# Two transformer blocks on one core: the residual stream kept as token rows, with output and down projections that hold the activations stationary

## The chip, the cores and the metric

The kernel runs on one core of a Trainium2 chip. The metric is the device time of one execution in microseconds (us). A core has a matrix engine (TensorE, PE in the profile), a vector engine (VectorE, DVE), a scalar engine (ScalarE, ACT), GpSimd (POOL) and a queue engine (SyncE, SP) that here issues the DMA transfers of the weights. Times of one run come from three executions; the profile is one more execution with the hardware profiler on.

## The reference

256 tokens of width 2048 pass two blocks, in float32. Block 1:

```
h = rmsnorm(x, norm_attn_pre);  proj = h @ w_in
mixed = concat(dilated window attention (8 heads), latent attention (8 heads))
x = x + rmsnorm(mixed @ w_out, norm_attn_post)
h = rmsnorm(x, norm_mlp_pre);  u = square(relu(h @ w_up))        # 2048 -> 8192
x = x + rmsnorm(u @ w_down, norm_mlp_post)                       # 8192 -> 2048
```

Block 2:

```
h = rms_norm(x, norm1_g);  proj = h @ w_in_2
mixed = concat(window attention (8 heads), bidirectional gated linear attention (4 heads))
x = x + mixed @ w_out_2
h = rms_norm(x, norm2_g);  u = conv3(h @ w_up_2);  gate, val = split(u)   # 2 x 5632 columns
x = x + (silu(gate) * val) @ w_down_2                                     # 5632 -> 2048
```

Each `rmsnorm` divides a token's 2048 values by the root of their mean square and multiplies by a gain vector, one gain for each channel. Three norms matter here: the one ahead of the first MLP ("norm 2", behind the post-norm of the attention), the one ahead of block 2 ("norm 3", behind the post-norm of the first MLP) and the one ahead of the second MLP ("norm 4").

## The kernel before

Every float32 operand is split in a high and a low part (`hi`, `lo`); a product of two operands is three matmuls: high by high, high by low, low by high. Weights are streamed: a DMA brings a raw tile of four K-chunks (128 rows by 512 columns each; three buffers), ScalarE copies two chunks at a time into `whi` (line 173), VectorE subtracts into `wlo` (line 174); two chunks so split are a "part", and three parts can be held. All projection matmuls are issued by `mm` on line 121, so the profile tells them apart by the name of the accumulation tile:

- `pb` (`proj_b`): the activations of 128 tokens are the stationary operand, 512 weight columns stream past; a K-chunk is 2 token blocks by 3 matmuls of 512 columns, and the result is token rows.
- `pa` (`proj_a`): the weights are stationary, 256 tokens stream past; a K-chunk is 4 x 3 matmuls of 256 columns, and the result is channel rows (channels on partitions).
- `pm` (`proj_m`): weights stationary, channel rows too. With `both`, the high weights meet the high and low activations side by side in one matmul of 512 columns, and the low weights the high activations in one of 256: 4 pairs a chunk. Without it, 12 matmuls of 256 columns.

The residual stream is held as channel rows, `xT`, two tiles of [128, 8, 256]. Both output projections write channel rows: three groups of 512 output channels by `proj_a`, the last one by `proj_m` in its 256-column form. Behind the last one come the sums of squares over channels (`Stats`, with `sps` matmuls against a column of ones), the power on GpSimd (`rstd`, line 180), and two matmuls that spread the row over the partitions (`spread`, tile `spr`). `post_norm` then computes chunk after chunk of the new residual and of `hT`, the normalised activations times the gain (`scaled_split`, lines 211 and 212), while the first matmuls that use them are under way. `hold_back` and `late` keep the first weight splits behind the norm's own instructions.

Each MLP starts with a wide group (1024 columns, 256-column matmuls, eight accumulators); all further up groups and the down projections are `proj_m` pairs, except the last down group, in the 256-column form. Block 1 runs its MLP in four parts of 16 chunks of the hidden width (`sb`), block 2 in three (16, 16, 12): up, then down into four groups, accumulated into `acc` or `xT`.

Attention work is cut in small steps, which a list (`Side`) issues between the parts of a projection (`tick`, `side.rate` steps per part); `flush` issues what is left. The output projection of a block needs the heads in the order of `MK`, four at a time (`need`), and flushes those. Instructions run in program order on each engine, and a scheduler inserts the waits. In block 2 the input projection's parts stand in this order: keys, queries and gates (`ka`, `kb`, `qg`) right behind norm 3, decay gates, the remaining `pb` groups for queries and values (`vg`, two blocks of 512 columns, the last before the output projection).

Of the kernel before, what the change touches and what calls it, by code (L numbers as in the profile page):

```python
# [10 lines left out]
F32 = mybir.dt.float32  # L11
# [8 lines left out]
P = 128  # L20
# [6 lines left out]
G_PRE1, G_CQ, G_CKV, G_POST1, G_PRE2, G_POST2, G_PRE3, G_PRE4, G_BAF, G_BAB, G_CW, G_CB = (  # L27
    0, 16, 20, 24, 40, 56, 72, 88, 104, 108, 112, 112 + 264)
G_N = 112 + 352
# [60 lines left out]
def tile_two_blocks(ctx: ExitStack, tc: tile.TileContext, a: dict, out: bass.AP):  # L90
# [3 lines left out]
    whl = ctx.enter_context(tc.tile_pool(name="whl", bufs=3))  # L94
    big = ctx.enter_context(tc.tile_pool(name="big", bufs=14))
# [3 lines left out]
    psb = ctx.enter_context(tc.tile_pool(name="psb", bufs=5, space=PSUM))  # L99
    pss = ctx.enter_context(tc.tile_pool(name="pss", bufs=3, space=PSUM))  # L100
# [4 lines left out]
    def scratch(shape, name, dt=F32):  # L105
        return scr.tile(shape, dt, tag="t2", name=name, bufs=12)
# [28 lines left out]
    nc.sync.dma_start(gains[:, :G_POST1], a["gains"][:, :G_POST1])  # L135
# [31 lines left out]
    late, held = [None, None], [0, 0]  # L167

    def hold_back():
        held[:] = 1, 2  # L170

# [4 lines left out]
    def rstd(ss, n, width):  # L176
        v = col(n, "v")
        late[1] = nc.vector.tensor_scalar(v, ss, 1.0 / width, EPS, op0=ALU.mult, op1=ALU.add)
        r = col(n, "r")
        nc.gpsimd.tensor_tensor(r, v, mhalf[:, :n], op=ALU.pow)  # L180
        return r
# [32 lines left out]
    def w_parts(nk, n, loads, pieces=1, first=False):  # L214
# [9 lines left out]
        for i in range(nk // h):  # L224
            if first:
                split_xT(i)
            hi = whl.tile([P, h, n], F32R, tag="hi", name="whi")
            lo = whl.tile([P, h, n], F32R, tag="lo", name="wlo")
            with ExitStack() as order:
                if held[0]:  # L230
                    held[0] -= 1
                elif held[1]:
                    held[1] -= 1
                    for ins in late:
                        order.enter_context(tc.issue_after(ins.ins))
                split(hi, lo, raw[:, i * h:(i + 1) * h])
            yield [(i * h + k, hi[:, k], lo[:, k]) for k in range(h)]
            side.tick()

    def proj(xT, ks, loads_of, ktile, before, pieces, body, both=False, final=False):  # L240
        nk = len(ks)
        for k0 in range(0, nk, ktile):
            kk = min(ktile, nk - k0)
            if before is not None:
                before(k0)
            parts = w_parts(kk, *loads_of(ks[k0], kk), pieces=pieces if k0 == 0 else 2 if pieces > 1 and k0 == ktile else 1,
                            first=pieces > 1 and k0 == 0)
            if final and k0 + kk == nk:
                parts = [[e for part in parts for e in part]]
            for part in parts:  # L250
                body([(k0 + k == 0, k0 + k == nk - 1, *hl(xT, ks[k0 + k]),
                       *([hl2(xT, ks[k0 + k])] if both else []), wh, wl) for k, wh, wl in part])

    def proj_b(xT, ks, loads_of, evac, n=512, before=None, pieces=1):
        ps = [bankb(f"pb{tb}") for tb in range(2)]

        def body(part):
            for first, last, xh, xl, wh, wl in part:
                for tb in range(2):
                    s = slice(tb * P, (tb + 1) * P)  # L260
                    o = ps[tb][:, :n]
                    mm(o, xh[:, s], wh, first, False)
                    mm(o, xh[:, s], wl, False, False)
                    mm(o, xl[:, s], wh, False, last)

        proj(xT, ks, loads_of, 4, before, pieces, body)
        for tb in range(2):
            evac(tb, ps[tb])

    def proj_a(xT, ks, loads_of, evac, n=512, ktile=4, before=None, pieces=1):  # L270
# [11 lines left out]
        proj(xT, ks, loads_of, ktile, before, pieces, body)  # L282
# [4 lines left out]
    def proj_m(xT, ks, loads_of, evac, n=512, both=True, before=None, final=False):  # L287
        if n == 512:
            turn[0] ^= both
            ps = [banks(f"pm{b}") if both and turn[0] and b < 3 else bankb(f"pm{b}") for b in range(4)]  # L290
            of = [p[:, :T] for p in ps]
        else:
            ps = [bankb(f"pm{b}") for b in range(4)]
            of = [p[:, m * T:(m + 1) * T] for p in ps for m in range(2)]
        alone = n == 512
        if not alone:
            turn[0] = 0

        def body(part):
            for m, o in enumerate(of):  # L300
                c = slice(m * P, (m + 1) * P)
                for first, last, xh, xl, xb, wh, wl in part:
                    if both:
                        mm(ps[m], wh[:, c], xb, first, last)
                        mm(ps[m][:, T:], wl[:, c], xh, False, last)
                    else:
                        mm(o, wh[:, c], xh, first and (alone or m % 2 == 0), False)
                        mm(o, wh[:, c], xl, False, False)
                        mm(o, wl[:, c], xh, False, last)

        proj(xT, ks, loads_of, 2048 // n, before, 1, body, both=True, final=final)
        for m, o in enumerate(of):
            evac(m, o, ps[m][:, T:] if both else None)
# [52 lines left out]

    def cols2(r):
        return [r[:, 0:1], r[:, 1:2]]
# [96 lines left out]
    nc.sync.dma_start(gains[:, G_POST1:], a["gains"][:, G_POST1:])  # L465
# [224 lines left out]
    xT = [slot([P, 8, T], F32, f"xr{j}") for j in range(2)]  # L690
    for j in range(2):
        nc.sync.dma_start(xT[j], a["xt"][j * 1024:(j + 1) * 1024, :].rearrange("(k p) t -> p k t", p=P))

    def bank3(ps):
        return ps.rearrange("p (m t) -> p m t", t=T)

    class Stats:
        def __init__(self):
            self.i = 0

        def add(self, src):
            i = self.i
            self.i += 1
            if i % 2 == 0:
                self.sq = scratch([P, 2, T], "sq")
            sq = self.sq
            if i == NC - 1 and src.space != PSUM:
                nc.vector.tensor_mul(sq[:, i % 2], src, src)
            else:
                late[0] = nc.scalar.activation(sq[:, i % 2], src, AF.Square)  # L710
            if i == NC - 1:
                token_sum(self.ps, [sq[:, 1]], False, True)
                return self.ps[:, 0:2]
            if i == NC - 2:
                self.ps = banks("sps")
                token_sum(self.ps, [self.acc[:, 0], sq[:, 0]], True, False)
            elif i == 1:
                self.acc = sq
            elif i % 2:
                nc.vector.tensor_add(self.acc, self.acc, sq)  # L720
            if i == NC - 3:
                nc.vector.tensor_add(self.acc[:, 0], self.acc[:, 0], self.acc[:, 1])

    def post_norm(xT, yT, row, g0, dst, wide):
        for c, n in ((0, 1), (1, 1), (2, 1), (3, 1), *((c, 2) for c in range(4, NC, 2))):
            t = scratch([P, n, T], "pn")
# [618 lines left out]
```

## Time and profile before

| | |
|---|---|
| device time, median of 3 | 2194.13 us (2193.82 to 2195.15) |
| the profiled execution | 2196.3 us |
| its span, first to last instruction | 2194.5 us |
| granted TensorE clock, mean | 0.995 |
| busy: PE, DVE, ACT, POOL | 2175.1, 1391.7, 1088.0, 16.0 us |
| DMA | 396.14 MB, mean 181 GB/s |

A clock of 1.00 means that TensorE was granted its full 2.4 GHz, 0.5 that it was at 1.2 GHz. Matmuls overlap: the durations in a row of the timeline overlap their neighbours, and the distance from one start to the next is what a matmul costs in a stream. A piece of the chain of waits that holds many matmuls gives that distance as its length over its count. The last of several matmuls in a piece is followed by the start of the next piece.

### The profile page before, as it was taken

Reading aid. Unit: us, or ns where it says so; the run is one execution under the profiler, and the core shown is the slowest. Engines: PE = TensorE matmul, PEld = TensorE weight load, DVE = VectorE, ACT = ScalarE, POOL = GpSimd, SP = SyncE. Lnnn points to the kernel's source line nnn. Section 1 sums busy time; section 2 is a strip of 40 time slices with the busy share of each in tenths; the row PEclk is TensorE's granted clock in tenths of the full one; section 3 lists DMA queues with packets and bytes.
Section 4 is the critical chain, followed back from the end, with each engine's and each line's share of the span. In section 5 each row is a group of like instructions: output and inputs, shape, how many; then the busy total and the mean of one; then the engine's idle time right before and its main releaser. Section 6 shows DMA issues by size and latency. Waiting matters only on the chain.

```text
span 2194.5 us, 32879 instructions
## 1 busy us (share of the span) xinstructions
PE 2175.1 (99%) x13298; PEld 1943.2 (89%) x13298; DVE 1391.7 (63%) x2115; ACT 1088.0 (50%) x1578; POOL 16.0 (1%) x22
## 2 busy tenths in 40 slices
PE   8999999999999999999999999999999999999999
PEld 8988899988888888888898889998888888888888
DVE  7665565764565565566678775566765567655765
ACT  6554454644443444344466565445553455534553
POOL 0000000000000000000000000000000000000000
PEclk9999999999999999999999999999999999999999
DMA  7545644555655665665454543545555555555555
GB/s 258 164 135 184 201 172 164 170 195 192 191 190 187 187 189 190 191 192 193 146 186 154 176 162 115 182 166 180 191 187 182 188 192 181 184 192 185 180 192 154
DMA packets 249641, 396.14 MB, mean 181 GB/s; under 512 B 12784, under 2 KB 107888, under 8 KB 249488
## 3 DMA queue, kind: packets, MB, share of 16 engines
q1 hardware_dynamic: 249488, 394.03, 55.5%
q8 instruction: 104, 1.70, 0.3%
q14 instruction: 49, 0.40, 0.0%
HBM read 391.90 MB, written 2.10 MB: 180 GB/s over the span
## 4 chain that ended last, share of the span: by engine, by line
PE 96%; DVE 2%; DMA 1%; ACT 1%; issue 0%; POOL 0%; SPq 0%; POOLq 0%; ACTq 0%
PE pm L121 69%; PE pb L121 11%; PE pa L121 8%; PE qg L121 1%; DMA raw<-in_w_in 1%; PE uq L121 1%; PE sc L121 1%; DVE wlo L174 1%; PE ka L121 1%; PE pv L121 1%; PE pk L121 1%; PE kb L121 0%; PE po L121 0%; ACT whi L173 0%; PE wsc L121 0%
## 5 line engine op out<-in xcount | busy, mean ns | idle before, releaser
L174 DVE TENSOR_TENSOR wlo<-raw,whi 128x1024 fp32r<-128x1024 f32 (+2 forms) x758 | 902.8, 1193 | 676.2 <-ACT whi L173 673.4
L173 ACT CAST whi<-raw 128x1024 fp32r<-128x1024 f32 (+2 forms) x758 | 776.6, 1026 | 938.5 <-PE pm L121 700.4
L121 PE MATMUL pm<-hT,whi 128*128 128x512 f32 (+1 forms) x2688 | 860.9, 376 | 2.5 <-ACT hT L211 1.5
L121 PE MATMUL pm<-hT,wlo 128*128 128x256 f32 x2432 | 684.9, 282 | 0.0
L121 PE MATMUL pm<-u,whi 128*128 128x512 f32 (+1 forms) x1840 | 605.2, 381 | 0.0
L121 PEld LDWEIGHTS pm<-hT,whi 128*128 128x128 f32 x2688 | 491.9, 190 | 100.4 <-ACT hT L211 1.7
L121 PE MATMUL pm<-u,wlo 128*128 128x256 f32 x1728 | 484.7, 281 | 0.0
L121 PEld LDWEIGHTS pm<-hT,wlo 128*128 128x128 f32 x2432 | 462.5, 190 | 0.0
L121 PEld LDWEIGHTS pm<-u,whi 128*128 128x128 f32 x1840 | 337.6, 188 | 70.2
L121 PEld LDWEIGHTS pm<-u,wlo 128*128 128x128 f32 x1728 | 326.7, 189 | 0.0
L121 PE MATMUL pb<-whi,hT 128*128 128x512 f32 x768 | 246.0, 395 | 0.1
L121 PEld LDWEIGHTS pb<-whi,hT 128*128 128x128 f32 x768 | 144.2, 188 | 29.5 <-DVE nr_t L892 0.5
L121 PE MATMUL pb<-wlo,hT 128*128 128x512 f32 x384 | 151.4, 394 | 0.2 <-DVE wlo L174 0.2
L121 PE MATMUL pa<-mix,whi 128*128 128x256 f32 x768 | 141.3, 286 | 0.0
L121 PEld LDWEIGHTS pa<-mix,whi 128*128 128x128 f32 x768 | 120.3, 192 | 0.9 <-DVE mix L1196 0.4
L121 PE MATMUL pa<-mix,wlo 128*128 128x256 f32 x384 | 108.5, 284 | 0.1
L121 PEld LDWEIGHTS pb<-wlo,hT 128*128 128x128 f32 x384 | 72.2, 188 | 15.7 <-DVE wlo L174 1.8
L121 PE MATMUL pa<-hT,whi 128*128 128x256 f32 x384 | 72.4, 290 | 5.6 <-ACT whi L173 5.4
L121 PEld LDWEIGHTS pa<-mix,wlo 128*128 128x128 f32 x384 | 73.5, 192 | 0.3 <-DVE wlo L174 0.3
L121 PEld LDWEIGHTS pa<-hT,whi 128*128 128x128 f32 x384 | 61.0, 196 | 7.4 <-ACT whi L173 6.6
L1253 ACT ACTIVATE gv<-us,gains 128x256 f32<-128x256 f32 x80 | 46.0, 601 | 27.9 <-DVE us L1276 27.2
L121 PE MATMUL pa<-hT,wlo 128*128 128x256 f32 x192 | 54.9, 289 | 1.0 <-DVE wlo L174 1.0
(289 smaller groups left out, 1594.6 us busy)
## 6 DMA issues: line engine op xcount, KB each, us to landing
raw<-in_w_down SPq DMA_DIRECT2D x108, 1024.0 KB, 5.0
raw<-in_w_up SPq DMA_DIRECT2D x176, 512.0 KB, 4.1
raw<-in_w_up SPq DMA_DIRECT2D x64, 1024.0 KB, 5.5
raw<-in_w_in SPq DMA_DIRECT2D x62, 1024.0 KB, 5.2
raw<-in_w_out SPq DMA_DIRECT2D x32, 1024.0 KB, 5.1
raw<-in_w_ukv SPq DMA_DIRECT2D x4, 1024.0 KB, 5.1
raw<-in_w_uq SPq DMA_DIRECT2D x4, 768.0 KB, 4.6
raw<-in_w_in SPq DMA_DIRECT2D x4, 544.0 KB, 3.7
```

The source lines that it names most:

```text
L121: nc.tensor.matmul(ps, lhsT, rhs, start=start, stop=stop, skip_group_check=True)
L173: nc.scalar.copy(hi, src)
L174: return nc.vector.tensor_sub(lo, src, hi.bitcast(F32))
L1253: nc.scalar.activation(dst, ps, AF.Identity, bias=b, scale=w[1])
```

## The change

The residual stream is kept as token rows: `xN[tb]`, one tile of [128 tokens, 2048] for each of the two token blocks. `proj_a` stays only in input projections. All projections whose result is added to the residual run as `proj_b`, and the last group of each one that precedes a norm as `proj_last`: its last eight K-chunks (`TRAIL`) are multiplied first for token block 0, then that block is evacuated and its norm is computed (`chain`), then the same eight chunks run for block 1. The normalised rows are transposed by TensorE (`flips`, line 125, tiles `fl`), four 128 x 128 pieces at a time, between the first eight chunks of the next projection, which runs as `proj_first`. The up projections' first group of each MLP is such a `proj_first` too; its output rows are transposed afterwards (`flip_rows`, tiles `fl` and `fu`). All other up groups are `proj_m` pairs. There are 112 such transposes in the program.

The gains of norms 2 and 4 are multiplied into the weights while these are split (`fold`: a `scaled_split` for each K-chunk of 512 columns in place of one `split` for two chunks). The gain of norm 3 is applied in the transposes' copies, in pieces of 128 columns. The gains of the post-norms are rows, broadcast over the partitions (`gp`). Sums of squares come from ScalarE's accumulated `Square` per 512 columns.

In block 2, the first `vg` block is multiplied right behind norm 3 (`proj_first`), the residual is written to DRAM (`x2`) and read back ahead of the second `vg` block, and the gated linear attention's steps are flushed ahead of that one. The split tiles have six buffers in place of three; the pool of 8 KB slots has 12 in place of 14, and that of scratch tiles 10 in place of 12. The output leaves as token rows.

The core of the diff:

```
-    whl = ctx.enter_context(tc.tile_pool(name="whl", bufs=3))
-    big = ctx.enter_context(tc.tile_pool(name="big", bufs=14))
+    whl = ctx.enter_context(tc.tile_pool(name="whl", bufs=6))
+    big = ctx.enter_context(tc.tile_pool(name="big", bufs=12))
...
+            r = raw[:, i * h:(i + 1) * h]
+            if fold is None:
+                split(hi, lo, r)
+            else:
+                for k in range(h):
+                    scaled_split(hi[:, k], lo[:, k], r[:, k], gain(fold + i * h + k))
...
+    TRAIL = LEAD = 8
+
+    def proj_last(xT, ks, loads_of, evac, done0=None, mid=None, before=None):
+        ps = [bankb(f"pb{tb}") for tb in range(2)]
+        held, k = [], 0
+        for part in stream(xT, ks, loads_of, before=before):
+            if k < len(ks) - TRAIL:
+                for e in part:
+                    for tb in range(2):
+                        rows_mm(ps, tb, [e])
+            else:
+                rows_mm(ps, 0, part)
+                held.append(part)
+            k += len(part)
+        evac(0, ps[0])
+        if done0:
+            done0()
+        for i, part in enumerate(held):
+            if i == len(held) - 1 and mid:
+                mid()
+            rows_mm(ps, 1, part)
+        evac(1, ps[1])
+
+    def proj_first(xT, ks, loads_of, flips, evac, n=512, fold=None):
+        ps = [bankb(f"pb{tb}") for tb in range(2)]
+        parts = stream(xT, ks, loads_of, fold=fold)
+        got = [next(parts), next(parts)]
+        flips(0, 1)
+        rows_mm(ps, 0, got[0], n)
...
+        rows_mm(ps, 0, got[3], n)
+        flips(1, 1)
+        rows_mm(ps, 1, got[0], n)
...
+    def flipper(hT, src_of, g0=None):
+        def flips(tb, j):
+            ps = banks("fl")
+            src = src_of(tb, j)
+            for i in range(4):
+                flip(ps[:, i * P:(i + 1) * P], src[:, i * P:(i + 1) * P], i == 0)
...
+            if g0 is None:
+                split(hi, lo, pv)
+            else:
+                for i in range(4):
+                    scaled_split(hi[:, i], lo[:, i], pv[:, i], gain(g0 + 4 * j + i))
...
+        def chain(self, tb):
+            r = last_rstd(self.ss[tb][:, 3:4], self.pre[tb])
+            for j in range(4):
+                x = self.xN[tb][:, col4(j)]
+                nc.vector.scalar_tensor_tensor(x, self.yg[tb][:, col4(j)], r, x, op0=ALU.mult, op1=ALU.add)
...
         if g < 3:
-            proj_a(mix, MK, cols_of(a["w_out"], g * 512), evac, before=need)
+            proj_b(mix, MK, cols_of(a["w_out"], g * 512), evac, before=need)
         else:
-            proj_m(mix, MK, cols_of(a["w_out"], g * 512), evac_m, both=False, before=need, final=True)
+            proj_last(mix, MK, cols_of(a["w_out"], g * 512), evac, lambda: post.chain(0), lambda: flips(0, 0))
+            post.chain(1)
...
+            if end and g == 3:
+                proj_last(u, range(SB), cols, evac, lambda: post.chain(0), lambda: flips(0, 0))
+                post.chain(1)
+            else:
+                proj_b(u, range(SB), cols, evac)
...
+    proj_first(hT, range(NC), cols_of(w_in2, 2560), flips, vg0.__setitem__)
...
-    for blk in range(2):
-        proj_b(hT, range(NC), cols_of(w_in2, 2560 + blk * 512),
...
-        side.flush([f"g{h}" for h in range(4)])
-        for h in (2 * blk, 2 * blk + 1):
-            side.add(8 + h, gla_out(h))
+    side.flush([f"g{h}" for h in range(4)])
+    for h in range(2):
+        side.add(8 + h, gla_out(h))
+    proj_b(hT, range(NC), cols_of(w_in2, 3072),
```

How TensorE's instructions stand in the program, at three places. First, in the first MLP's down projection. `u` holds the hidden activations, `whi` and `wlo` the split weights; the name left of the arrow is the accumulation tile, right of it stand the operands, stationary one first in no fixed order. Before:

```order
L121 MATMUL pm_4938<-u_3754,whi 128x512
L121 MATMUL pm_4938<-u_3754,wlo 128x256
L121 MATMUL pm_4938<-u_3754,whi 128x512
L121 MATMUL pm_4938<-u_3754,wlo 128x256
L121 MATMUL pm_4939<-u_3754,whi 128x512
L121 MATMUL pm_4939<-u_3754,wlo 128x256
L121 MATMUL pm_4939<-u_3754,whi 128x512
L121 MATMUL pm_4939<-u_3754,wlo 128x256
```

After:

```order
L122 MATMUL pb_4413<-whi,u_3370 128x512
L122 MATMUL pb_4413<-wlo,u_3370 128x512
L122 MATMUL pb_4413<-whi,u_3370 128x512
L122 MATMUL pb_4412<-whi,u_3370 128x512
L122 MATMUL pb_4412<-wlo,u_3370 128x512
L122 MATMUL pb_4412<-whi,u_3370 128x512
```

What were eight matmuls a chunk, four pairs of 512 and 256 columns with the weights stationary, are six of 512 columns, three for each token block (`pb_4412`, `pb_4413`).

Second, from the first block's output projection (`mix`) into the first MLP (`hT`), where `sps`, `one` and `sq` belong to the sum of squares, `spr` and `r` to the spread of its root, and `fl` and `xn` to the transposes of the normalised rows. Before:

```order
L121 MATMUL pm_3487<-mix_0_2832,whi 128x256 x2
L121 MATMUL pm_3487<-mix_0_2832,wlo 128x256
L121 MATMUL sps<-one,sq 128x1 x6
L121 MATMUL spr<-ident,r 128x128 x2
L121 MATMUL pm_3756<-hT_3739,whi 128x256
L121 MATMUL pm_3757<-hT_3739,whi 128x256
L121 MATMUL pm_3758<-hT_3739,whi 128x256
L121 MATMUL pm_3759<-hT_3739,whi 128x256
L121 MATMUL pm_3756<-hT_3739,whi 128x256
L121 MATMUL pm_3756<-hT_3739,wlo 128x256
```

After:

```order
L122 MATMUL pb_3198<-whi,mix_0_2784 128x512
L125 MATMUL fl<-ident,xn_2622 128x128 x4
L122 MATMUL pb_3198<-whi,mix_0_2784 128x512
L122 MATMUL pb_3198<-wlo,mix_0_2784 128x512
L122 MATMUL pb_3198<-whi,mix_0_2784 128x512 x2
L122 MATMUL pb_3198<-wlo,mix_0_2784 128x512
L122 MATMUL pb_3198<-whi,mix_0_2784 128x512
L125 MATMUL fl<-ident,xn_2622 128x128 x4
L122 MATMUL pb_3374<-whi,hT_2634 128x512
L122 MATMUL pb_3374<-wlo,hT_2634 128x512
L122 MATMUL pb_3374<-whi,hT_2634 128x512 x2
L122 MATMUL pb_3374<-wlo,hT_2634 128x512
```

The sum and the spread are gone from TensorE, the first transposes stand ahead of the last two parts of block 1's trailing chunks, and further ones between the first chunks of the up projection.

Third, in block 2's output projection (`mix`), with the window attention's scores (`wsc`), transposes (`wpt`) and outputs (`wpo`). Before:

```order
L124 MATMUL wpt<-ident,we 128x128
L121 MATMUL pa_12443<-mix_0_12402,whi 128x256
L124 MATMUL wpt<-ident,we 128x128 x3
L121 MATMUL pa_12443<-mix_0_12402,wlo 128x256
L121 MATMUL pa_12443<-mix_0_12402,whi 128x256 x2
L121 MATMUL pa_12443<-mix_0_12402,wlo 128x256
L121 MATMUL pa_12443<-mix_0_12402,whi 128x256
L124 MATMUL wpt<-ident,we 128x128
L121 MATMUL pa_12443<-mix_0_12402,whi 128x256
L124 MATMUL wpt<-ident,we 128x128 x3
L121 MATMUL pa_12443<-mix_0_12402,wlo 128x256
L121 MATMUL wpo<-wpT,kv_10202 128x256 x4
```

After:

```order
L122 MATMUL pb_11397<-whi,mix_0_11128 128x512
L125 MATMUL hT<-ident,nat 128x128 x8
L122 MATMUL wsc<-kv_9476,qaT 128x256 x4
L125 MATMUL wpt<-ident,we 128x128 x8
L122 MATMUL wpo<-wpT,kv_9476 128x256 x4
L122 MATMUL wsc<-kv_9476,qaT 128x256 x4
L122 MATMUL pb_11396<-whi,mix_0_11511 128x512
```

Where projection matmuls stood between the window attention's steps, the steps of the last heads follow one another, and the projection's next chunk (`pb_11396`) comes behind them.

## Rows read from the trace of the kernel before

**Rows 1.** The page: busy share of the engines, and the chain's lines.

```profile
PE 2175.1 (99%) x13298; PEld 1943.2 (89%) x13298; DVE 1391.7 (63%) x2115; ACT 1088.0 (50%) x1578; POOL 16.0 (1%) x22
...
PE pm L121 69%; PE pb L121 11%; PE pa L121 8%; PE qg L121 1%; DMA raw<-in_w_in 1%; PE uq L121 1%; PE sc L121 1%; DVE wlo L174 1%; PE ka L121 1%; PE pv L121 1%; PE pk L121 1%; PE kb L121 0%; PE po L121 0%; ACT whi L173 0%; PE wsc L121 0%
```

**Rows 2.** Chain of waits: start us, us, what, with its count of instructions.

```profile
196.15 21.35 PE pb L121 x94
...
460.64 627.74 PE pm L121 x3680
...
1362.49 51.38 PE pa L121 x426
...
1413.87 23.05 PE pm L121 x192
...
1441.84 749.61 PE pm L121 x4400
```

**Rows 3.** Windows, TensorE only: stretch, us, busy (count), granted clock, DMA share, GB/s.

```profile
640.00:800.00 160.00, 160.00 (x925) 1.00 0.59 190
1500.00:1700.00 200.00, 200.00 (x1133) 1.00 0.58 187
```

**Rows 4.** Timeline of TensorE: start us, us, engine, line, operation, tiles, shapes, count.

```profile
1700.17 0.40 PE L121 MATMUL pm<-u,whi 128*128 128x512 f32 x1
1700.41 0.28 PE L121 MATMUL pm<-u,wlo 128*128 128x256 f32 x1
1700.53 0.40 PE L121 MATMUL pm<-u,whi 128*128 128x512 f32 x1
```

**Rows 5.** Transposes: the chain, the groups by line and the window 114 to 268.

```profile
1349.83 0.87 PE ogT L124 x8
...
L124 PE MATMUL hT<-ident,nat 128*128 128x128 f32 x32 | 5.0, 278 | 0.0
...
114.00:268.00 154.00, 154.00 (x733) 1.00 0.56 178
```

**Rows 6.** The norms: the chain, and the window 1088 to 1101, all engines.

```profile
367.18 1.25 PE sps L121 x12
...
368.69 0.70 POOL r L180
...
371.66 88.63 PE pm L121 x608
...
1094.12 1.27 PE ka L121 x4
...
1135.08 3.00 PE kb L121 x24
1138.09 5.74 PE qg L121 x48
...
1088.00:1101.00 13.00, 9.86 (x59) 9.28 (x58) 8.67 (x21) 4.65 (x10) 1.04 (x1) 0.74 0.15 44
```

**Rows 7.** Window attention on the chain: score, projection and output matmuls.

```profile
1261.03 1.73 PE wsc L121 x8
1262.75 7.26 PE pb L121 x32
...
1272.14 0.87 PE wpo L121 x4
```

**Rows 8.** Groups by line, 1255 to 1345: busy, mean ns, idle before.

```profile
L174 DVE TENSOR_TENSOR wlo<-raw,whi 128x1024 fp32r<-128x1024 f32 x26 | 31.7, 1222 | 15.3 <-ACT whi L173 15.2
L173 ACT CAST whi<-raw 128x1024 fp32r<-128x1024 f32 x26 | 27.2, 1048 | 28.0 <-PE pb L121 22.1 <-PE pa L121 4.5 <-issue 1.2
...
L1103 DVE SCALAR_TENSOR_TENSOR ws<-wsc,cb_t 128x512 f32<-128x512 f32 x8 | 5.5, 688 | 6.0 <-PE wsc L121 6.0
...
L1132 ACT COPY wpT<-wpt 128x512 f32<-128x512 f32 x8 | 4.7, 582 | 1.6 <-PE wpt L124 1.6
```

**Rows 9.** Window in the second MLP: busy PE, PEld, DVE, ACT, POOL, clock, DMA.

```profile
1530.00:1620.00 90.00, 90.00 (x512) 78.07 (x511) 61.72 (x88) 49.65 (x72) 0.00 (x0) 1.00 0.58 187
```

More of the change, by code (lines that the diff above doesn't have):

```diff
@@ L228, in w_parts, with stream @@
             lo = whl.tile([P, h, n], F32R, tag="lo", name="wlo")
[L229 to L236, printed above, removed]
+            r = raw[:, i * h:(i + 1) * h]
[4 more added lines that the diff above has]
+                    scaled_split(hi[:, k], lo[:, k], r[:, k], gain(fold + i * h + k))
             yield [(i * h + k, hi[:, k], lo[:, k]) for k in range(h)]
             side.tick()
-    def proj(xT, ks, loads_of, ktile, before, pieces, body, both=False, final=False):
+    def stream(xT, ks, loads_of, ktile=4, before=None, pieces=1, both=False, fold=None):
         nk = len(ks)
@@ L245, in proj @@
                 before(k0)
[L246 to L252, printed above, removed]
@@ L254, in proj_b @@
-    def proj_b(xT, ks, loads_of, evac, n=512, before=None, pieces=1):
+            for part in w_parts(kk, *loads_of(ks[k0], kk),
+                                pieces=pieces if k0 == 0 else 2 if pieces > 1 and k0 == ktile else 1,
+                                first=pieces > 1 and k0 == 0, fold=None if fold is None else fold + k0):
+                yield [(k0 + k == 0, k0 + k == nk - 1, *hl(xT, ks[k0 + k]),
+                        *([hl2(xT, ks[k0 + k])] if both else []), wh, wl) for k, wh, wl in part]
@@ L259, in body @@
                 for tb in range(2):
[L260 to L266, printed above, removed]
+                    rows_mm(ps, tb, [e], n)
         for tb in range(2):
             evac(tb, ps[tb])
+    TRAIL = LEAD = 8
[4 more added lines that the diff above has]
+            if k < len(ks) - TRAIL:
+                for e in part:
+                    for tb in range(2):
[12 more added lines that the diff above has]
+        evac(1, ps[1])
@@ L280, in body, with proj_m @@
                     mm(o, wl[:, c], xh, False, last)
-        proj(xT, ks, loads_of, ktile, before, pieces, body)
+        for part in stream(xT, ks, loads_of, ktile, before, pieces):
+            body(part)
         evac(ps)
     turn = [0]
[L287 to L300, printed above, removed]
+    def proj_m(xT, ks, loads_of, evac, fold=None):
+        turn[0] ^= 1
+        ps = [banks(f"pm{b}") if turn[0] and b < 3 else bankb(f"pm{b}") for b in range(4)]
+        for part in stream(xT, ks, loads_of, both=True, fold=fold):
+            for m in range(4):
                 c = slice(m * P, (m + 1) * P)
                 for first, last, xh, xl, xb, wh, wl in part:
[L303 to L313, printed above, removed]
+                    mm(ps[m], wh[:, c], xb, first, last)
+                    mm(ps[m][:, T:], wl[:, c], xh, False, last)
+        for m in range(4):
+            evac(m, ps[m][:, :T], ps[m][:, T:])
     def cols_of(w, c0, n=512):
@@ L687, in tile_two_blocks @@
             side.add(4 * blk + h, dswa(4 * blk + h))
[L690 to L722, printed above, removed]
@@ L809, in tile_two_blocks @@
[L809 to L813 removed]
+                nc.scalar.copy(t, cross)
+                nc.vector.tensor_add(t, main, t)
+                nc.vector.scalar_tensor_tensor(uf, t, 0.0, t, op0=ALU.max, op1=ALU.mult)
+                split(*hl(u, 4 * g + m), uf)
```

399 lines of the change are left out of this document (230 added, 169 removed).

## The prediction

> **What bounds the kernel now.** I read the page's busy shares first, then its chain of waits, then the chain piece by piece, and at last windows and timelines of the stretches that the change touches. The busy shares show TensorE at work 99% of the span, VectorE 63%, ScalarE 50%; the chain that ended last is matmuls, 69% of it in tiles named pm and 11% in pb [rows 1]. So time is won here by shorter matmul streams or by closing the few gaps between them, and a longer list on another engine costs only where a matmul waits for it.
>
> What a stream costs is read from undisturbed chain pieces [rows 2]. A 512-column matmul with activations stationary (pb): 21.35 us over 94, so 227.1 ns, and a K-chunk of 128 rows by 512 columns, six of them, costs 1.362 us. A 256-column one: 23.05 over 192 (pm) and 51.38 over 426 (pa), so 120 ns, twelve per chunk, 1.440 us. The streaming alone would be 213.3 and 106.7 ns at 2.4 GHz, so each matmul carries some 13.5 ns more, whatever its width. The third form, pairs of 512 and 256 columns (8 matmuls a chunk), has two paces. In 640 to 800 us there are 925 matmuls in 160 us, 346 ns a pair; in 1500 to 1700 us 1133 in 200 us, 353 ns [rows 3]. The long chain pieces agree: 627.74 us less 192 matmuls of 0.120 leaves 604.7 for 436 chunks, 1.387 each; 749.61 us less 528 of 0.120 leaves 686.2 us for 484 chunks, 1.418, of which the windows' 353 ns a pair makes 1.413 and a low clock at its start the rest, 2.3 us [rows 2, 3]. In the slower pace the 512-column matmul takes 0.24 us and its partner 0.12 [rows 4].
>
> **The change part by part.** The sum is made against the profiled execution, 2196.3 us (span 2194.5 and 1.8 around it), which is 2.2 over the median of the runs, 2194.13.
>
> a. Output and down projections become pb. First down projection: 240 chunks from 1.387 to 1.362, 6.0 us. Second: 164 from 1.413 to 1.362, 8.4. The last group of each, 28 chunks of 256-column matmuls, and both output projections, 128 chunks: 156 by 0.078, 12.2. Together **-26.6**. All of it lies on the path, since TensorE is never without work there.
>
> b. Up projections. The wide first groups (64 chunks at 1.440) go; the first group of each MLP becomes pb (32 chunks in all at 1.362), the other 576 chunks stay pairs. Before: 64 x 1.440 + 32 x 1.413 + 192 x 1.387 + 320 x 1.413 = 855.9 us. After: 43.6 + 576 x 1.387 = 842.5, or with 1.413, 857.5. So **-13.4 or +1.6**, by which pace the pairs take. The trace says little on that: the pace was slow twice behind a stream of 256-column matmuls and quick from 460.64 us to 1088 us, right behind a short wait of TensorE; within a stretch it never changed. After the change each run of up groups starts behind pb matmuls, several times over, so I take half of the groups in either pace, **-5.9**, and keep both ends.
>
> c. New transposes on TensorE (fl, fu): 112. Eight stood in 0.87 us [rows 5], 109 ns each: **+12.2**.
>
> d. The norms. Now TensorE stands still three times while sums of squares, the power on GpSimd (0.70 us), the spread of the result and the first normalised chunk are waited for. Ahead of the first MLP: last projection matmul done at 367.18, first up matmul at 371.66, 4.5 us; the 384 matmuls of 120 ns and 28 chunks of 1.413 behind it would be 85.7 us and took 88.63, so 3.0 more under a low clock. Ahead of block 2: 1088.4 (the end of the long piece) to 1143.8 is 55.4 us for 192 qg matmuls of 0.1196 and 192 ka and kb matmuls of 0.125, 47.0; 8.4 lost, with a granted clock of 0.74 in the first 13 us. Ahead of the second MLP: 1436.9 to 1441.84, 4.9, and 2.3 behind it (749.61 less 528 x 0.120 and 484 x 1.413). Sum 23.1 [rows 2, 6]. After the change token block 0 is finished eight chunks early, and its sum, power, scaling and first transposes run beside block 1's eight trailing chunks (8 x 3 x 227 = 5.4 us). What must fit into the first three quarters of that, 4.1 us: a square or product of 512 columns (0.69), a small sum (0.2), the power (0.70), one 512-column product (0.69), with waits of about 1 us, some 3.3 us [rows 6, 8]. So at the first and the third of these norms I leave 2 us each. At the second the gain stays in the transposes' copies: eight groups of four 128-column copies on ScalarE (0.4 us each is my estimate from the 0.58 of 512 columns that the transposes' copies take [rows 8] and a fixed part of about 0.35), 12.8 us, and four casts of 1.05, against 8 chunks by 1.362 = 10.9 of matmuls: some 6 us left. Gain 23.1 - 10 = **-13**. If nothing were hidden, 0; if all, -23.
>
> e. The second block's output projection. Before, the window-attention steps of heads 4 to 7 had a value projection between them: from the score matmuls at 1261.03 to the first output matmul at 1272.14, 32 pb matmuls filled 7.26 us [rows 7]. The first block of that projection now runs right behind the norm ahead of block 2, the steps are carried on less often, and in the new order score, transpose and output matmuls of the last heads follow each other with no projection matmul between. The steps between them on the other engines are two scores' products of 0.69, a maximum, an exponential and a copy of 0.58 [rows 8]: about 5.3 us idle at the first, 2.2 and 0.5 at the next: **+8**. Bounds: 3 if the products of one head are done while the other's scores run; 14 if the idle stretch also costs clock, as the 3 us behind the first norm did.
>
> f. Gains in the weight splits. A split of 1024 columns on ScalarE (1.05 us) and VectorE (1.22) becomes two of 512 (0.58 to 0.69 each) [rows 8]. In 1530 to 1620 us VectorE is 69% busy and ScalarE 55% [rows 9]; a seventh more on what is mostly splits makes about 76% and 66%: both still run ahead of the matmuls, and six buffers in place of three give more slack. Cost **0**; without that cover a split of 1.38 on VectorE every 2.75 us would still not bind. Where a pb group follows an up group that holds four of the five large banks, it waits up to 1 us for an evacuation, three times at the most: **+1**. The residual's way to DRAM and back (2 MB each) is issued far ahead of use: 0. Row-wise residual additions replace channel-wise ones of the same size: 0.
>
> Sum: -26.6 - 5.9 + 12.2 - 13 + 8 + 1 = -24.3: 2172 for the profiled execution, 2169.8 beside the median. **Forecast 2169 us.**
>
> **A rule beside it.** The extra time of each matmul is 13.5 ns in both widths [rows 2]. The Trainium skill, TensorE: Matmul & The Clock Gate, section "Back-to-back issue gap", gives the isolated gap as columns over 2.4 GHz plus about 2.5 ns, by which 512 columns would take 215.8 ns and two of 256 columns 218.4: a and the wide part of b would then bring about 1,980 x 2.5 ns = 5 us, not 32. The rows show 13.5 ns in long runs of either form, so the sum goes by them.
>
> **Rivals.**
> 1. All pairs quick (1.387): b is -13.4, time 2162. For it: the longest busy stretch, 628 us, had that pace. Against: two of three stretches had the other.
> 2. All pairs slow (1.413): b is +1.6, time 2177. For it: 750 us of the second MLP; against: the stretch from 460 us.
> 3. Boundaries under a low clock: waits and transposes at the three norms and at the window steps bring the granted clock to half for some us each. For it: 0.74 in 13 us at 1088 [rows 6]. If each of four places loses 4 us more than in d and e, 2185. Against: 114 to 268 us has 32 transposes of one tile (hT) among its matmuls at a clock of 1.00 [rows 5]. The same page of the Trainium skill, section "Part 4: PE-mode transpose", says that transposes do not count as busy for the clock, and that one takes about 275 ns in a kernel; the rows' mean of one is 278 with overlap, but its place in the stream costs 109, and the clock beside them stayed full.
> 4. Slower: pb with u stationary takes its 512-column matmuls at the 0.24 us [rows 4] that they take in the slow pairs, not 0.227. Some 3,550 matmuls (2592 down, 768 output, 192 first groups) by 10 ns is 35 us: 2204. The even point is 234 ns. For it: that step exists in this kernel; against: all pb pieces here, 94 in a row, run at 227.
> 5. The 2.5 ns rule above holds, since what makes up the 13.5 ns lies elsewhere than in the count: a and b give 5 in place of 32, 2197. No row speaks for it.
> 6. The staggering hides all of d and the window steps interleave: 2154 to 2159.
>
> **How the numbers follow.** Chances: forecast 0.42, rival 1 0.2, rival 2 0.17, rival 3 0.1, rival 4 0.05, rival 5 0.02, rival 6 0.04. The forecast's own range is 2164 to 2175. The range of 8 in 10 goes from 2153 (rival 1 with more of d hidden) to 2187 (rival 3, or rival 2 with e at its upper end). What a measurement can tell from no change is 0.2%, 4.4 us, so faster means under 2189.7 and slower over 2198.5. Slower: rival 4 and a tail of rival 3, 0.06. Same: rival 5 and the other tail of 3, 0.04. Faster 0.9.
>
> **What would show it.** In the changed profile: pb pieces at 227 ns a matmul in both down projections (a; at 237 rival 4); pm pieces at 1.387 or 1.413 a chunk, group by group (b); groups fl and fu of four in 0.44 us (c); TensorE's idle time within 6 us of each norm's first transposes, largest at the second norm, behind ScalarE (d); idle before wpt and wpo at the start of the second output projection, behind VectorE and ScalarE, near 8 us in all (e); VectorE under 80% busy in the second MLP with no matmul waiting for wlo (f). Granted clock under 0.9 in several windows of 10 us around these places would mean rival 3. The prediction is wrong if the time is outside 2153 to 2187, and its reason is wrong if pb does not run at 227 ns or if the matmuls of the MLPs wait for the folded splits.

## The result, and the profile after

The changed kernel takes 2173.49 us (median of 4 runs, 2172.29 to 2174.32) against 2193.98: the ratio is 0.9906, with a 95% interval of 0.9888 to 0.9923. Its profiled execution took 2173.41 us, span 2171.5 us, granted clock 0.999; that of before 2196.3, so 22.9 us less between the two profiles. Between the medians it is 20.5, since the profiled execution of before was one of its slower ones (granted clock 0.995; the others listed have 0.995 to 0.998). The forecast was 2169 (2172 for a profiled execution), the range 2153 to 2187.

The page answers [rows 1]: TensorE has as large a share of a shorter span, and pb has taken most of pm's share of the chain.

```profile
PE 2151.4 (99%) x11290; PEld 1835.1 (85%) x11290; DVE 1387.8 (64%) x2235; ACT 1160.6 (53%) x1862; POOL 16.8 (1%) x25
...
PE pb L122 47%; PE pm L122 37%; PE pa L122 2%; PE qg L122 1%; DMA raw<-in_w_in 1%; PE uq L122 1%; PE sc L122 1%; PE ka L122 1%; PE kb L122 1%; DVE wlo L170 1%; PE pv L122 1%; PE pk L122 1%; PE po L122 0%; PE wpo L122 0%; DVE xn L787 0%
```

The chain through the MLPs (start us, us, what) answers [rows 2]. Divide each length by its count: 226.7 ns for every pb piece, and for the pairs 354 ns (22.48 over 63.5 pairs) at 389.03, 346.3 ns (44.15 over 127.5) at 412.75 and 353.3 ns from 543.98 us on. So 32 of the 576 pair chunks ran at the quick pace of 1.387 us, and 544 at 1.413.

```profile
389.03 22.48 PE pm L122 x127
412.75 44.15 PE pm L122 x255
456.90 87.08 PE pb L122 x384
543.98 90.44 PE pm L122 x512
634.42 87.06 PE pb L122 x384
...
1464.69 146.99 PE pm L122 x832
1611.67 87.10 PE pb L122 x384
1698.78 180.89 PE pm L122 x1024
```

Norm 2 on the chain answers the sps, POOL and pm pieces of [rows 6]. VectorE's scaling and splits end at 364.4 us, and then chunks of matmuls (six in 1.38) alternate with transposes (four in 0.44):

```profile
360.43 2.07 DVE xn L787 x3
362.50 1.32 DVE wlo L208 x2
363.83 0.61 DVE hT L170
...
364.48 1.19 PE pb L122 x4
365.67 0.44 PE fl L125 x4
366.11 1.38 PE pb L122 x6
```

The chain passes through VectorE there, but TensorE had block 1's trailing chunks to do until 363.3 us: in 345 to 389 one step between starts is 0.54 us (from 363.94, ahead of the matmul that VectorE's `hT` releases) and no other is over 0.34, where a matmul in a stream takes 0.23. (The first transposes stand ahead of the last part of the trailing chunks, six matmuls, and not of the last two parts as the description says.) At norm 3 it does wait. This is the timeline (start us, us, engine, line, ..., idle before and its releaser):

```profile
1081.21 0.62 ACT L354 ACTIVATE junk<-xn 128x512 bf16<-128x512 f32 x1
...
1081.73 0.19 ACT L354 ACTIVATION_READ_ACCUMULATOR junk<-xn 128x1 f32 x1
1081.83 0.36 ACT L207 ACTIVATE hT<-fl,gains 128x128 fp32r<-128x128 f32 x1
1082.08 0.62 ACT L354 ACTIVATE junk<-xn 128x512 bf16<-128x512 f32 x1
1082.31 0.34 DVE L208 SCALAR_TENSOR_TENSOR hT<-fl,gains,hT 128x128 fp32r<-128x128 f32 x1
...
1082.71 0.50 PE L122 MATMUL pb<-whi,hT 128*128 128x512 f32 x1 [0.61 <-DVE hT L208]
```

The squares of L354 (the sums for `r3`) stand behind this whole projection in the code, and ran between the transposes' copies: the scheduler had moved them there, so the words "in program order" of the description above hold for the order that it leaves, not for that of the code.

The granted clock (the figure ahead of the last two in a row) was full at all three norms after, and at half behind each of them before. After:

```profile
345.00:389.00 44.00, 43.86 (x209) 1.00 0.57 176
1065.00:1108.00 43.00, 40.65 (x186) 1.00 0.51 169
1418.00:1440.00 22.00, 21.76 (x111) 1.00 0.42 137
```

Before:

```profile
371.10:377.80 6.70, 6.14 (x28) 6.14 (x29) 5.42 (x11) 2.29 (x4) 0.00 (x0) 0.50 0.44 153
1091.30:1098.00 6.70, 5.10 (x21) 4.81 (x22) 4.75 (x13) 1.42 (x3) 0.03 (x1) 0.50 0.29 86
1439.50:1446.20 6.70, 5.58 (x24) 5.29 (x25) 5.33 (x11) 1.59 (x4) 0.06 (x1) 0.50 0.15 30
```

Block 2's output projection, the window's row and the chain (it answers [rows 7] for heads 4 to 7):

```profile
1320.00:1330.00 10.00, 6.35 (x26) 4.97 (x25) 5.69 (x17) 4.36 (x14) 0.00 (x0) 0.83 0.34 108
```

```profile
1318.58 1.15 PE wsc L122 x4
1319.75 0.70 DVE ws L1152
1320.47 0.69 DVE wm L1155
1321.16 0.60 DVE ws L1152
...
1322.22 0.99 ACT we L1165 x4
...
1324.13 1.09 PE wpt L125 x4
```

From the scores at 1318.6 to the transposes at 1324.1 every step waits for the one before it on another engine, TensorE is busy 6.35 of 10 us, and its granted clock falls to 0.83 in that window. Before, the scores of these heads stood ahead of the projection, whose first matmul started at 1331.65:

```profile
1312.66 1.99 PE wsc L121 x8
```

How the time went, by stretches. "Lost" is the length of a stretch, from start to start, less its matmuls at their streaming price (227 ns for 512 columns, 120 for 256, 125 for 272 and 109 for a transpose). Row b is 32 chunks at 1.360, 32 at 1.387 and 544 at 1.413 us, 856.6, less the 855.9 of before:

| | forecast | measured |
|---|---|---|
| a. down and output projections | -26.6 | -27.4 |
| b. up projections | -5.9 | +0.7 |
| c. 112 transposes | +12.2 | +12.2 |
| d. norms 2, 3, 4: lost 6.9, 8.1, 6.5 before; 0.8, 5.6, 0.9 after | -13 | -14.2 |
| e. output projection of block 2: lost 5.4, now 15.7 | +8 | +10.3 |
| f. splits with gain, banks | +1 | 0 |
| the rest of block 2's attention: lost 12.5, now 8.4 | 0 | -4.1 |
| sum, against 22.9 to 23.0 between the profiles | -24.3 | -22.5 |

Of the 4.1 us in the last row ahead of the sum, 2.5 are the scores, products and output matmuls of the last four heads, which stood in the stretch ahead of the output projection before and stand in it now. Like with like, e is +7.8 and the rest -1.6.

### The profile page after: what moved, and what is told of

It is laid out like the page before. It is cut to its first block, busy times and chain, and to the rows that moved or that the text cites. A ratio compares the mean times of both kernels' runs of the same rounds, so it can differ in the third digit from the quotient of the medians.

```text
span 2171.5 us, 29093 instructions
## 1 busy us (share of the span) xinstructions
PE 2151.4 (99%) x11290; PEld 1835.1 (85%) x11290; DVE 1387.8 (64%) x2235; ACT 1160.6 (53%) x1862; POOL 16.8 (1%) x25
## 4 chain that ended last, share of the span: by engine, by line
PE 95%; DVE 2%; DMA 1%; issue 1%; ACT 1%; SPq 0%; POOL 0%; POOLq 0%; DVEq 0%; ACTq 0%
PE pb L122 47%; PE pm L122 37%; PE pa L122 2%; PE qg L122 1%; DMA raw<-in_w_in 1%; PE uq L122 1%; PE sc L122 1%; PE ka L122 1%; PE kb L122 1%; DVE wlo L170 1%; PE pv L122 1%; PE pk L122 1%; PE po L122 0%; PE wpo L122 0%; DVE xn L787 0%
## 5 line engine op out<-in xcount | busy, mean ns | idle before, releaser
L122 PE MATMUL pm<-hT,whi 128*128 128x512 f32 x2304 | 813.8, 398 | 0.0
L170 DVE TENSOR_TENSOR wlo<-raw,whi 128x1024 fp32r<-128x1024 f32 (+2 forms) x454 | 530.8, 1173 | 441.3 <-ACT whi L169 438.4
L169 ACT CAST whi<-raw 128x1024 fp32r<-128x1024 f32 (+2 forms) x454 | 457.6, 1011 | 550.7 <-PE pb L122 406.3
L208 DVE SCALAR_TENSOR_TENSOR wlo<-raw,gains,whi 128x512 fp32r<-128x512 f32 x608 | 437.0, 747 | 234.2 <-ACT whi L207 231.4
L207 ACT ACTIVATE whi<-raw,gains 128x512 fp32r<-128x512 f32 x608 | 413.9, 718 | 293.6 <-PE pm L122 199.1
L122 PE MATMUL pb<-whi,u 128*128 128x512 f32 x1728 | 533.7, 389 | 0.0
L122 PEld LDWEIGHTS pb<-whi,u 128*128 128x128 f32 x1728 | 324.4, 188 | 67.7
L122 PE MATMUL pb<-wlo,u 128*128 128x512 f32 x864 | 336.2, 389 | 0.0
L122 PEld LDWEIGHTS pb<-wlo,u 128*128 128x128 f32 x864 | 162.2, 188 | 33.2
L122 PE MATMUL pb<-whi,mix 128*128 128x512 f32 x512 | 162.1, 393 | 0.0
```

What stands on the lines that cost most here:

```text
L122: nc.tensor.matmul(ps, lhsT, rhs, start=start, stop=stop, skip_group_check=True)
L169: nc.scalar.copy(hi, src)
L170: return nc.vector.tensor_sub(lo, src, hi.bitcast(F32))
L207: nc.scalar.activation(hi, src, AF.Copy, scale=g)
L208: return nc.vector.scalar_tensor_tensor(lo, src, g, hi.bitcast(F32), op0=ALU.mult, op1=ALU.subtract)
```

## The experiments

All were made from the changed kernel, 2173.5 us. "Before" is 2194.5 in their comparisons, 2194.0 in that of the changed kernel; executions of one kernel differ by 0.5 to 4.4 us, so differences of 1 to 3 us are believed here only where the traces show them too. The code is cut at "...".

**e1: runs of one width.**

```
                 for first, last, xh, xl, xb, wh, wl in part:
                     mm(ps[m], wh[:, c], xb, first, last)
+            for m in range(4):
+                c = slice(m * P, (m + 1) * P)
+                for first, last, xh, xl, xb, wh, wl in part:
                     mm(ps[m][:, T:], wl[:, c], xh, False, last)
```

> The changed kernel, with the up projections' pairs taken apart: of a part (two K-chunks) first the eight 512-column matmuls, then the eight 256-column ones. Theory: the 353 ns of a pair is a lock of the alternation 512, 256, 512, 256; in runs of one width each takes its own 227 and 120 ns, so 528 chunks go from 1.413 to 1.387 us and the time from 2173.5 to about 2160. Rival: the 353 ns belongs to the work itself (loads of high and low weights), whatever the order: 2173, and a chunk stays at 1.41.

2164.92 us, ratio to before 0.9866 (0.9851 to 0.988): 8.6 faster than the changed kernel, two thirds of what the theory said (its 528 slow chunks are 544). Eight 512-column matmuls and eight of 256 in its timeline:

```profile
1520.54 2.00 PE L122 MATMUL pm<-hT,whi 128*128 128x512 f32 x8
1522.38 1.12 PE L122 MATMUL pm<-hT,wlo 128*128 128x256 f32 x8
1523.33 0.40 PE L122 MATMUL pm<-hT,whi 128*128 128x512 f32 x1
```

From start to start the eight wide ones take 1.84 us, 230 ns each, and the eight narrow ones 0.95, 119 each. Singly, the first five behind the change of width step by 229 to 235 ns, the last three by 227. In the pairs at the slow pace the wide ones step by 232 to 241. So the order does set the price, and the rival falls; but a change from narrow to wide has a price of its own, here 27 ns. A chunk came to 145.26 us over 104, 1.397:

```profile
1462.03 145.26 PE pm L122 x832
```

**e9 and e10: a break at the start of a run.** Four transposes at six places in `proj_m`, in e9 behind the first 512-column matmul, in e10 ahead of it.

```
                     mm(ps[m], wh[:, c], xb, first, last)
+                    if kick and first and m == 0:
+                        for i in range(4):
+                            flip(ps[3][:, i * P:(i + 1) * P], ident, i == 0)
                     mm(ps[m][:, T:], wl[:, c], xh, False, last)
...
```

> The changed kernel with four transposes of the identity (into a bank that is started afresh afterwards) at six places: in the first pair of the up projections' runs behind a down projection (block 1 from its second part on, block 2's second and third part) and of one group early in block 2's first part, between the 512-column and the 256-column matmul. Theory: the pace of the pairs is a lock that outlasts groups and is set where a run starts; the one quick run of the changed kernel began with transposes ahead of a 256-column matmul. So all six runs turn quick: 512 chunks x 0.026 = 13.4, less 6 x 0.44 = 2.6 for the transposes: 2162 to 2164. Rival: the pace comes from the data or the banks of a run, and the transposes are pure cost: 2176.

> As e9, with the same four transposes one matmul earlier, ahead of the first pair's 512-column matmul. Theory: only a run that starts again with a 256-column matmul is quick, one that starts with 512 columns is slow as in all starts behind pb: 2175.5 to 2177. Rival: any disturbance of this length makes the pairs quick: as e9, 2162 to 2164.

e9: 2169.58 us, 0.9884 (0.987 to 0.9897), between its two expectations. e10: 2176.89 us, 0.9917 (0.9904 to 0.9931), as its theory said. In e9 three of the six runs became quick. The chain shows it for the three in block 1, of which only the middle one did:

```profile
546.11 90.22 PE pm L122 x511
...
724.06 88.53 PE pm L122 x511
...
900.34 90.22 PE pm L122 x511
```

In e10 none of six did. So the pace is a lock and not a matter of data or banks: the run at 724.06, quick in e9 with 88.53 us, has the same operands and accumulators in e10 and took 90.45 us there.

Transposes ahead of a narrow matmul can turn it. The changed kernel has such a place too, eight transposes of `flip_rows` at 411.4 to 412.5 us: behind them the pairs became quick in the changed kernel and in e2, e3, e4, e7 and e12, but stayed slow in e9 and e10. In e8 the same transposes fell ahead of 512-column matmuls, and the pairs stayed slow. Transposes ahead of a wide matmul turned the pace in none of these runs. But the width behind the break is not the whole rule, for the kernel before turned at 460.5 us inside a run of slow pairs, at four one-column matmuls ahead of a wide one:

```profile
460.13 0.50 PE L121 MATMUL st<-one,sq 128*128 128x1 f32 x4
460.50 0.48 PE L121 MATMUL pm<-hT,whi 128*128 128x512 f32 x1
```

What decides stays open.

**e7: part of the down projection in pairs.** For `sb` below 3:

```
+            if not end:
+                def evac_m(m, main, cross):
...
+                proj_m(u, range(SB), cols, evac_m)
+            elif end and g == 3:
```

> The changed kernel with three quarters of the first MLP's down projection (192 of 256 K-chunks) back in the pair form with the weights stationary; what it yields is channel rows put into the token-row accumulator, so that these values are not the reference's. Theory: term a is the price of the form alone: 192 x (1.413 - 1.361) = 10 us more at the slow pace of the pairs, 2183.5; at the quick pace 5 more, 2178.5. Rival: the gain of the down projections came from their surroundings (evacuations of token rows, banks): within 2 us of 2173.5, or over 2188.

2174.05 us, 0.9904 (0.9891 to 0.9918). That is the rival's number, but not for its reason. All pairs of block 1 from 411.89 us on were quick, up and down, one piece of 1.387 us a chunk:

```profile
411.89 576.64 PE pm L122 x3327
988.54 81.65 PE pb L122 x360
```

So 192 down chunks cost 192 x (1.387 - 1.361) = 5.0 more, and 192 up chunks, slow in the changed kernel, 192 x 0.026 = 5.0 less: they cancel, and the time is the same within 0.6. So for these 192 chunks term a is the price of the form, as forecast; and what the pb stretches take away here is the quick pace of the pairs behind them.

**e2: no stagger.** In `proj_last` both blocks run chunk by chunk, and `evac(0)`, `done0()`, `evac(1)`, `mid()` follow.

> The changed kernel without the trailing chunks: the last groups run both token blocks chunk by chunk, block 0's evacuation and norm come after the last matmul; the transposes between the first chunks of the next projection stay. Theory: the staggering hides a chain of 3 to 5 us at each of three norms, so 2173.5 + 9 to 15 = 2183 to 2189, with idle time of TensorE right behind each last group and a lower granted clock there. Rival: what pays at the norms is that the sums and spreads left TensorE, and transposed rows of one block are enough to go on: 2175 at the most.

2183.85 us, 0.9951 (0.9936 to 0.9966): 10.4 slower, as the theory said. Lost at the three norms: 3.6, 7.9 and 5.1 us behind the last matmuls, 16.6 in all against 7.3, and the granted clock was 0.91 in 1074 to 1094. Against the 21.5 of before, 4.9 us of the gain remain without the stagger. Norm 3 on its chain: TensorE's last matmul started at 1078.47 and its next, a transpose, at 1083.71, and VectorE's scaling stands ahead of that one.

```profile
1078.90 1.05 ACT whi L169
...
1079.97 1.23 DVE wlo L170
1081.20 0.60 DVE acc L874
...
1082.01 0.86 POOL lr L344
...
1082.90 2.74 DVE xn L785 x4
```

**e4: gain of norm 3 in the splits.** `flipper(hT, post.src)` without gain, `fold=G_PRE3` in all of block 2's input projections.

> The changed kernel with the gain of norm 3 in block 2's weight splits too, as at norms 2 and 4, so that the transposes' copies there are one of 512 columns in place of four of 128. Theory: of the 6 to 7 us that TensorE loses at norm 3, 3 to 5 are these small copies on ScalarE and VectorE: 2168.5 to 2170.5. Rival: the loss there is the sums of squares and other work that the two engines do at that place, and the longer splits add to it: 2173 to 2177.

2171.09 us, 0.9895 (0.9878 to 0.9911): 2.4 faster. Lost at norm 3: 2.1 in place of 5.6; the stretch up to the output projection gives 1.2 of it back (9.7 in place of 8.5), with longer splits. Between the two expectations: without the small copies most of norm 3's loss is gone.

**e3: heads 4 to 7 last.**

```
+                for e in [e for e in self.todo if e[0] in keys or str(e[0])[0] in "qk"][:WIDTH]:
...
-    MK = list(range(NC))
+    MK = [0, 1, 2, 3, 8, 9, 10, 11, 12, 13, 14, 15, 4, 5, 6, 7]
```

The first line belongs to `flush`, which now issues only the steps asked for.

> The changed kernel with heads 4 to 7 of the window attention taken last in block 2's output projection (K-chunks 0-3, 8-15, 4-7 in place of 0 to 15), and a flush that issues only the steps asked for. Theory: the 10 us that TensorE lost more in this projection is latency of steps with no projection matmul between them; with twelve chunks ahead of them part of it is covered: 2165 to 2169. Rival: ScalarE and VectorE are the bound of this stretch, and the idle time only moves to the last four chunks: 2172 to 2174.

2168.19 us, 0.9881 (0.9866 to 0.9895): 5.3 faster, with both edits; neither was tried alone. The output projection lost 10.4 in place of 15.7, and in no window of 10 us from 1315 to 1355 was the granted clock under 1.00:

```profile
1315.00:1325.00 10.00, 8.30 (x44) 6.50 (x43) 5.08 (x11) 4.87 (x13) 1.39 (x2) 1.00 0.59 210
1325.00:1335.00 10.00, 10.00 (x47) 8.50 (x46) 6.98 (x14) 4.59 (x13) 0.00 (x0) 1.00 0.02 5
1335.00:1345.00 10.00, 9.26 (x48) 7.21 (x47) 6.47 (x14) 5.44 (x14) 1.40 (x2) 1.00 0.29 103
```

**e8: splits without gain.** `split` in place of `scaled_split` in `w_parts`.

> The changed kernel with plain splits in the up projections, so the gains of norms 2 and 4 are left out. Theory: the folded splits are hidden but for the first parts of each MLP: 2172.5 to 2173.5. Rival: ScalarE and VectorE, each an eighth to a seventh longer at it, set the pace at the norms or in the second MLP: 2168 or less.

2174.75 us, 0.991 (0.9896 to 0.9923): 1.3 slower, outside both expectations and hardly more than the spread of the executions. No cost of the folded splits is seen: TensorE is busy without a break in both rows below. In 1530 to 1600 us they take VectorE from 69% to 75% busy and ScalarE from 54% to 65% (e8 first, the changed kernel second):

```profile
1530.00:1600.00 70.00, 70.00 (x399) 60.68 (x398) 48.39 (x70) 37.98 (x55) 0.00 (x0) 1.00 0.57 188
```

```profile
1530.00:1600.00 70.00, 70.00 (x398) 60.67 (x397) 52.23 (x93) 45.21 (x80) 0.00 (x0) 1.00 0.56 182
```

What the trace shows for the 1.3 us are two small things: a split of 1.22 us can't be interrupted, and two of them stand ahead of the first `hT` on VectorE at norm 2 (lost 1.2 in place of 0.8), and the pairs from 412 to 457 us stayed slow (see e9), 0.8.

**e5, e6, e11, e12: together.** e5 is e1, e3 and e4; e6 adds runs of 16 (two parts are collected) and three side steps per part; e11 has the runs of 16 alone; e12 has e9's transposes in place of the runs.

> The changed kernel with the three edits of the first series together: runs of one width in the up projections, heads 4 to 7 last with a flush of what is asked for, gain of norm 3 in the weight splits. Theory: they act at three separate places of TensorE's stream, so their savings of 8.6, 5.3 and 2.4 us add: 2157 (2155.5 to 2158.5). Rival: two of them share a wait (the splits with gain make ScalarE later where the heads need it): 2160 or more.

> The three edits together, with runs of 16 matmuls of one width (two parts) in place of 8, and three steps of attention work per part in place of two from the second value block of block 2 on. In the runs of 8 the 512-column matmuls take some 230 ns on the mean and the first five behind a change of width are the slow ones; theory: a change of width costs some 27 ns, so half as many changes give 528 chunks x 0.007 = 3 us, and the earlier window steps 1 to 3 us more: 2151 to 2154. Rival: longer runs need two parts split ahead and make a matmul wait for a split, and steps issued earlier only stand in the way: 2157 or more.

> The three edits of e5 together, with runs of 16 matmuls of one width, and the attention steps at their old rate of two. Theory: in e6 the longer runs gained some 2 us and the third step per part lost them again in block 2's projections: 2155 to 2156.5. Rival: the longer runs gain nothing: 2157 to 2158.5.

> Heads 4 to 7 last, gain of norm 3 in the weight splits, and e9's transposes in place of the runs of one width. Theory: if e9's pairs are quick at 1.387, the savings add to 2173.5 - 10.5 - 5.3 - 2.4 = 2155 to 2156. Rival: the pairs fall back to the slow pace within the runs: 2160 to 2168.

| | us | ratio to before |
|---|---|---|
| e5 | 2157.77 | 0.9833 (0.9819 to 0.9846) |
| e6 | 2158.23 | 0.9834 (0.9821 to 0.9848) |
| e11 | 2154.89 | 0.9818 (0.9805 to 0.9832) |
| e12 | 2160.71 | 0.9845 (0.9831 to 0.9858) |

e5: the three savings add up to 16.3, measured 15.7. e11 against e5: the longer runs gained 2.9, and its up chunks take 1.391 us in place of 1.397. e6: the third step lost this again in the stretches before the output projection (235.7 us from the last down matmul to its first one, against 231.95 in e11). e12: four of six runs became quick; the time is in the range of the rival, but no run fell back, two never turned. e11 is the best version, 18.6 us under the changed kernel and 39.7 under before. Its second MLP's pairs, 178.11 us for 1024, are 1.391 a chunk:

```profile
1452.73 144.74 PE pm L122 x832
...
1684.54 178.11 PE pm L122 x1024
```

## Why the prediction was right, and where its terms were off

- **a and c** held as priced: 226.7 ns a matmul in every pb piece, four transposes in 0.44 us. Rival 4 fell with the first, and so did rival 5: a matmul takes 13.3 to 13.4 ns over its streaming time here, and 27.4 us came from a. By my estimate the rule of the Trainium skill (TensorE: Matmul & The Clock Gate, "Back-to-back issue gap") would have given about 5 us for a with the wide part of b; the trace, 226.7 and 120 ns, does not agree with it. (The 32 us that the prediction sets beside these 5 hold all of its b; the wide part alone is 3 to 4 us, and its 1,980 matmuls are 2,064.) e7 confirms the price of the form for 192 chunks of the first MLP.
- **b** is the term that was mis-sized, +0.7 for -5.9. I let half of the groups take either pace; 544 of 576 chunks ran at 1.413. The prediction leaned on a quick stretch that began behind a wait, and said that within a stretch the pace never changed. The trace of before says otherwise: the 28 chunks ahead of 460.5 us were slow, and the pace changed inside that run of pairs. What the same stretches had to say was that none had become quick without a break inside a run of pairs, and that the change would put a start behind a pb stretch seven times. This is rival 2 for that term; its 2177 is 3.5 us over the measured time, less than what the rest of block 2 gave.
- **d** held in sum, -14.2 for -13, with its parts off: norms 2 and 4 lose less than 1 us, not 2, and norm 3 5.6, for 6. e2 shows that 9 to 10 us of it hang on the trailing chunks, and e4 that 3.5 of the 5.6 left at norm 3 go with the small copies; the squares that the scheduler put between them were not tried apart. Part of what before lost was clock: its three stretches of 6.7 us at 0.50 are gone.
- **e** held, +10.3 for +8 (+7.8 like with like), the wait where it was said (5.5 us from scores to transposes), and with the loss of clock (0.83) of the upper bound for one window. e3 gives half of it back.
- **f** held: VectorE 75% and ScalarE 65% busy (forecast 76 and 66), though one folded half takes 0.75 and 0.72 us and not 0.58 to 0.69. In e8, without the fold, nothing is gained.
- What no step of the prediction had: the rest of block 2's attention lost 4.1 us less. 2.5 of it moved into e with the steps of the last heads; what gave the other 1.6 was not tried.
- So the mechanism of a, c, d and e was right, and the closeness of the sum is in part luck: b was 6.6 us too hopeful, and 4.1 that no term had, 1.2 more from d and 0.8 from a nearly made up for that and for the 2.3 more in e.
- **Rival 3** did not come: the granted clock was 1.00 at all three norms, thirty-two transposes in each, and fell in one place of 10 us. The rule of the same page of the Trainium skill, section "Part 4: PE-mode transpose", that transposes do not count as busy for the clock, is not seen to cost anything here, where matmuls stand between them. Rivals 1 and 6 fell too: 32 of 576 chunks were quick, and d and e still lose 7.3 and 15.7 us.

## What to carry to other kernels

Price a matmul stream by the length of a chain piece over its count, for each form and for each place, since the same form can run at two paces for hundreds of microseconds; a change that makes new starts of such a stream may change its pace. Where a moved step leaves small steps of several engines without matmuls between them, sum their latencies: that term was a third of what the whole change saved elsewhere. A long dependent chain at a norm is hidden by finishing half of the tokens some chunks early, if the other engines have nothing else to do at that place.

## What the runs showed of the hardware that was not expected

Alternating 512- and 256-column matmuls hold one of two paces, 346.6 or 353.3 ns a pair, and keep it across groups, banks and operands for 577 us (e7) and, in the kernel before, for over 600 us without a change. Transposes ahead of a 256-column matmul turned the slow pace into the quick one in 3 of 6 added places in e9 and 4 of 6 in e12, and in 6 of 8 kernels at `flip_rows` of block 1; ahead of a 512-column one in none of 6 (e10) nor in e8. Four one-column matmuls ahead of a 512-column one turned it in the kernel before. A pb stretch was followed by the slow pace in every run of pairs that got no such break. In runs of one width the 512-column matmuls behind a change of width are slow for five instructions, 27 ns together, and then run at 227.
